# A hybrid layer on one core: three blocks between recurrence blocks, 64-row gate matmuls, and gate projections as paired seven-product blocks

## The chip, the cores and the metric

The kernel runs on one core of a Trainium2 chip. The metric is the device time of one execution in microseconds (us); shown are the median, the lowest and the highest of three executions, and one execution that was also recorded by the hardware profiler.

The engines are called PE (matrix multiplications), ACT (activation functions, copies and casts), DVE (element by element arithmetic and scans), POOL, and SP, which here only issues DMA transfers. An engine works through its own instructions in the order in which they stand in the program and waits at an instruction until the data that it needs are there.

## The reference

One layer is computed for 1024 latent tokens of width 1024 and 256 context tokens. Cut to what matters here:

```
h = rms_norm(x) * (1 + scale) + shift            # latents; the same for the context
u_lru, z_lru, u_fft, z_fft, u_pool, z_pool, gates = split(h @ w_in)
xc   = depthwise_conv(u_lru)                     # latents and context
r, i = sigmoid(block_diag(xc, wa)), sigmoid(block_diag(xc, wx))   # 64 x 64 blocks, two directions
a    = exp(-8 r softplus(-lam));  b = sqrt(1 - a^2) * (i * xc)
h_t  = a_t h_{t-1} + b_t                         # forward and backward, started by the context
ya = ((h_f + h_b) * silu(z_lru)) @ proj_a
yb = (fourier_mix(u_fft) * silu(z_fft)) @ proj_b
yc = (pool_mix(u_pool) * silu(z_pool)) @ proj_c
g  = sigmoid(gates)                              # three times 1024 columns: g, h, i
out = rms_norm(x + gate * ((g0 ya + g1 yb + g2 yc) @ w_out))
```

## The kernel before

**Tiling.** Channels lie on the 128 partitions, tokens along the free axis; a 128-channel block of 1024 tokens is one tile. Every fp32 operand of a product is split into a high and a low part (`split`, L127: ACT casts the high part, DVE subtracts for the low one), and `mm3` (L190 to L195) makes a product of three matmuls, low weight by high data, high by low, high by high. A projection block (eight 128-channel slices, 1024 tokens) is two half-blocks of 24 matmuls with 512 columns.

**Stages.** First come sums for the norm of x, the products `z` of L360 and the scaled activations: DVE scales `x` in place (`x<-x,gsc,rstd`), ACT makes the high part `hh`, DVE the low part `hl`; in between stand the splits of the last of these weights, `wz6` and `wz7`. Then a list `units` sets PE's order: four `ZP` blocks; eight recurrence blocks `u0` to `u7` with four other blocks behind each, from the list `others` (`UF`, `UP`, `ZF` and the 24 gate-logit blocks `i`, `h`, `g`); the last four gate blocks between the pooling products `m0` to `m3`; the branch products `c`, `s`, `t`, `b`, the blocks `pa` and the output product.

**A recurrence block.** `taken_in` makes the convolution `xc` (one ACT instruction and three on DVE, latents, and `xcc` for the context), `parts` its high and low parts (`xs`), and PE multiplies by the block-diagonal weights `bd`: `gates_c` (L701, context, tile `bdc`), then `gate` for r and i in each direction (`bdr`, `bdi`). In `parts` the high part of 64 channels lies above their low part, so one 128-row matmul does two of the three products. ACT takes sigmoids of all of them, exponentials, tanh and square roots, and each change between these kinds is an ACT_TABLE_LOAD. DVE multiplies and runs the scans (L768). The table `AT` (L1151) says at which half-block, counted from the block's own, each piece is written down:

```
AT = (("w", 0), ("in_", 1), ("sp", 1), ("gc", 4), ("g0r", 4), ("sc", 4), ("g0i", 5), ("s0r", 5), ("g1r", 6),
      ("s0i", 6), ("g1i", 7), ("s1r", 7), ("s1i", 8), ("ec", 8), ("e0", 8), ("e1", 8), ("qc", 8), ("q0", 8),
      ("q1", 8), ("kc", 8), ("k0", 8), ("z", 8), ("k1", 9), ("y", 9))
```

**Order.** PE's instructions run in the order in which they are written. ACT, DVE and SP follow an order that a scheduler made when the program was built; only in the start stage and at the end they too follow the code. All DMA transfers to and from memory are issued by SP in one row, so a store that waits for its data holds back the loads behind it.

Of the kernel before, what the change touches and what calls it, by code (L numbers as in the profile page):

```python
# [7 lines left out]
F32 = mybir.dt.float32  # L8
# [20 lines left out]
def tile_hybrid_mixer(  # L29
# [44 lines left out]
    def r4(name, shape=(128, 1024), pool=None):  # L74
        return (pool or p4).tile(list(shape), F32R, tag="t4", name=name)
# [141 lines left out]


    def hs(k, h):
        return tuple(t[:, h * HALF:(h + 1) * HALF] for t in ht[k])  # L220

    def proj_half(o, w, h, ks=range(NK), **kw):
# [19 lines left out]
    with tc.manual_schedule(engines={ET.PE}):  # L242
# [100 lines left out]

        def h_scaled(k):
            stt(xt[k], xt[k], gsc[0][k], rstd, ALU.mult, ALU.mult)
            ht[k] = r4(f"hh{k}"), r4(f"hl{k}")
            act(ht[k][0], xt[k], bias=shc[0][k])

        def h_lo(k):
            stt(ht[k][1], xt[k], shc[0][k], f(ht[k][0]), ALU.add, ALU.subtract)  # L350
            xt[k] = None


        def wave(k, ws, src):
            for n in range(3):
                for nm, hi, lo in ws:
                    o = pacc_t[nm]
                    for h in range(2):
                        x = src[k][n == 2][:, H[h]]
# [303 lines left out]
        def lru(j):  # L663
            t = lrus[j] = {}

            def weights():
                wf = f2(f"bd{j}_f", (128, 4, 128))
                SP.dma_start(out=wf, in_=bdw[j])
                t["wh"], t["wl"] = r2(f"bd{j}_h", (128, 4, 128)), r2(f"bd{j}_l", (128, 4, 128))
                split(t["wh"], t["wl"], wf)  # L670

            def taken_in():
# [2 lines left out]
                t["x"] = f4(f"xc{j}")  # L675
                conv(t["x"], t.pop("ps"), T, j)


            def stack(o, d, x):
                a, b = LANES[x], LANES[1 - x]  # L680
                S.copy(o[a], d[a])
                tt(o[b], d[a], f(o)[a], ALU.subtract)

            def parts():
                t["xc"] = r2(f"xs{j}", (128, 2, TC))
                for x in DIRS:
                    stack(t["xc"][:, x, :], t["c"], x)
                for x in DIRS:
                    t["xs", x] = r4(f"xs{j}_{x}")
                    stack(t["xs", x], t["x"], x)  # L690

            def both(o, n, x):
                for m, w in enumerate((t["wl"], t["wh"])):
                    PE.matmul(out=o, lhsT=w[:, n, :], rhs=x, start=m == 0, stop=m == 1)  # L694
# [5 lines left out]

            def gates_c():  # L701
                o = t["oc"] = acc(f"bdc{j}")
                cs = t.pop("xc")
                for n in range(4):
                    both(o[:, n * TC:(n + 1) * TC], 2 * (n % 2) + n // 2, cs[:, n % 2, :])

            def gate(x, kind):
                o = t["o", x, kind] = acc(f"bd{kind}{j}_{x}")
                for h in range(2):
                    both(o[:, H[h]], 2 * x + (kind == "i"), t["xs", x][:, H[h]])  # L710
                if kind == "i":
                    t.pop(("xs", x))

            def sigmoid_c():
                g, o = f4(f"gc{j}"), t.pop("oc")
                t["gc"] = g
                for n in range(4):
                    x, kind = n % 2, "ri"[n // 2]
                    for d in DIRS:
                        act(g[LANES[x], (2 * (n // 2) + d) * TC:(2 * (n // 2) + d + 1) * TC],  # L720
                            o[LANES[d], n * TC:(n + 1) * TC], AF.Sigmoid, bias=bias(x, kind)[LANES[d]])
# [57 lines left out]
            def gated():  # L779
# [7 lines left out]
            P = lambda f, *a: lambda: f(*a)  # L787
            return dict(w=weights, in_=taken_in, sp=parts, gc=gates_c, sc=sigmoid_c, ec=exp_c, qc=sqrt_c, kc=scan_c,
                        z=z_load, y=gated, e0=P(exp, 0), e1=P(exp, 1), q0=P(sqrt, 0), q1=P(sqrt, 1), k0=P(scan, 0),
                        k1=P(scan, 1), **{f"g{d}{k}": P(gate, d, k) for d in DIRS for k in "ri"},  # L790
                        **{f"s{d}{k}": P(sigmoid, d, k) for d in DIRS for k in "ri"})


# [328 lines left out]
        units += ("c0 c1 s0 c2 s1 t0 c3 s2 t1 c4 s3 t2 c5 t3 c6 c7 b0 b1 b2 b3 b4 b5 b6 b7").split()  # L1122
        units += halves(*[f"pa{n}" for n in range(NK)])
        pos_of = {u: n for n, u in enumerate(units)}
        wkeys = []
        for u in units:
            if isinstance(u, tuple):
                if u[1] == 0:
# [3 lines left out]
        queue = Queue([item(k) for k in wkeys])  # L1132
        branch = {"m": MP, "s": S1, "t": S2, "c": lambda d: PB(1, d), "b": lambda d: PB(0, d)}


# [7 lines left out]
        for k in range(NK):  # L1143
# [4 lines left out]
        on(6, ctx_parts, 0)  # L1148
        on(6, ctx_parts, 1)
        on(8, decays)  # L1150
        AT = (("w", 0), ("in_", 1), ("sp", 1), ("gc", 4), ("g0r", 4), ("sc", 4), ("g0i", 5), ("s0r", 5), ("g1r", 6),  # L1151
              ("s0i", 6), ("g1i", 7), ("s1r", 7), ("s1i", 8), ("ec", 8), ("e0", 8), ("e1", 8), ("qc", 8), ("q0", 8),
              ("q1", 8), ("kc", 8), ("k0", 8), ("z", 8), ("k1", 9), ("y", 9))
# [5 lines left out]
        on(pos_of["g4", 0] - 2, load_poolw)  # L1159
        on(pos_of["g4", 0], load_dft)  # L1160
        on(pos_of["g5", 0], group_dft)
# [5 lines left out]
        on(pos_of["g6", 0], load_tabs)  # L1167
        on(pos_of["g7", 0], split_tabs)
# [7 lines left out]
        on(pos_of["g4", 0] - 40, load_sbg)  # L1176
        for d in range(NK):
            on(pos_of["g4", 0] - 38 + 2 * d, gate_step, d)
        on(A0, load_ident)
        on(A0 + 2, gate_rows)  # L1180
        for k in range(3):
# [4 lines left out]
        for st, unit in enumerate(units):  # L1186
            flush_stores(st)
            late = st + 1
            for p in ev.pop(st, ()):
                p()  # L1190
            if isinstance(unit, tuple):
# [150 lines left out]
def _layout(i):  # L1342
# [4 lines left out]
    x, cx = a["x"][0], a["ctx"][0]  # L1347
    w = a["w_in"][0]

    bd = np.stack([a["lru_wa"][0], a["lru_wx"][0]]).reshape(2, 2, 8, 2, 64, 64).transpose(2, 4, 3, 0, 1, 5)  # L1350
    bd = np.concatenate([bd.reshape(8, 64, 4, 128)] * 2, axis=1)
# [42 lines left out]
```

## Time and profile before

| | |
|---|---|
| median of three executions | 1008.72 us (1008.42 to 1010.2) |
| the profiled execution | 1009.21 us, its span 1007.1 us |
| PE busy | 988.1 us, 4572 matmuls |
| DVE busy | 598.6 us |
| ACT busy | 537.3 us, of it 71 table loads 91.1 us |
| mean granted clock of PE | 0.997 |

The span is the recorded part of the execution, 2.1 us shorter than its time. A matmul's listed duration is longer than the distance to the next one, since matmuls overlap; the pace is read from the starts. A row "x2" is two instructions alike, with the time of both. In brackets stands the idle time of the engine ahead of an instruction and what ended it.

### The profile page before, as it was taken

To read this page: it belongs to the slowest core of one execution; us is meant where nothing else is said; L and a number is where in the kernel's file an instruction comes from. 1 tells how busy PE (TensorE), PEld (TensorE's weight loads), DVE (VectorE), ACT (ScalarE), POOL (GpSimd) and SP (SyncE) were. 2 spreads that over 40 slices of the span, in tenths; PEclk is the share of its full clock that TensorE was granted. 3 is DMA by queue.
4 is the path that set the end of the run, shared out by engine and by line. 5 is a ranking of instruction groups with operands and counts; after the bars stand their busy time and mean duration, and the time that the engine had idled before them with its cause. 6 is when DMAs were issued, how large, how long until landed. Compare 5 with 4: busy or idle time off the path is not lost.

```text
span 1007.1 us, 11592 instructions
## 1 busy us (share of the span) xinstructions
PE 988.1 (98%) x4572; PEld 816.9 (81%) x4572; DVE 598.6 (59%) x763; ACT 537.3 (53%) x632; POOL 21.6 (2%) x22
## 2 busy tenths in 40 slices
PE   7988999999999999999999999999999999999997
PEld 4867788888888888888888888887888888888886
DVE  6969266549465595653936537275566674456164
ACT  4453554595875948769596693954332222123031
POOL 0000000000000000000000000000000000000341
PEclk9999999999999999999999999999999999999999
DMA  9541495232322322334332233437545684324272
GB/s 341 210 157 43 147 411 237 73 105 84 109 90 94 105 96 88 137 140 147 136 138 92 74 105 136 135 118 283 170 173 212 244 318 157 138 83 136 73 250 75
DMA packets 47655, 152.58 MB, mean 152 GB/s; under 512 B 5489, under 2 KB 8177, under 8 KB 47602
## 3 DMA queue, kind: packets, MB, share of 16 engines
q1 hardware_dynamic: 47458, 151.59, 42.2%
q8 instruction: 36, 0.59, 0.2%
q10 hardware_dynamic: 144, 0.26, 0.1%
q14 instruction: 17, 0.14, 0.0%
HBM read 114.08 MB, written 37.75 MB: 151 GB/s over the span
## 4 chain that ended last, share of the span: by engine, by line
PE 82%; ACT 3%; DVE 2%; DMA 1%; issue 1%; SPq 0%; DVEq 0%; ACTq 0%
PE o L195 3%; PE o L194 3%; PE o L193 3%; PE ppa L195 3%; PE ph L194 3%; PE ppa L193 3%; PE ph L195 3%; PE pu L194 3%; PE pi L195 3%; PE ph L193 3%; PE pu L195 3%; PE pu L193 3%; PE pi L194 3%; PE pi L193 3%; PE ppa L194 3%; PE p L193 3%
## 5 line engine op out<-in xcount | busy, mean ns | idle before, releaser
L114 ACT ACT_TABLE_LOAD x71 | 91.1, 1283 | 2.0 <-PEq L1384 0.7
L120 DVE SCALAR_TENSOR_TENSOR junk<-ada,sb 128x1024 bf16<-128x1024 f32 x32 | 39.1, 1221 | 26.0 <-DMA ada<-in_ada 26.0
L194 PE MATMUL o<-wo_l,mh 128*128 128x512 f32 (+1 forms) x136 | 51.2, 377 | 0.0
L195 PE MATMUL o<-wo_h,mh 128*128 128x512 f32 (+1 forms) x136 | 51.2, 376 | 0.0
L193 PE MATMUL o<-wo_h,ml 128*128 128x512 f32 (+1 forms) x136 | 51.2, 376 | 0.0
L193 PE MATMUL pg<-hh,g_l 128*128 128x512 f32 x128 | 50.2, 392 | 0.0
L193 PE MATMUL ppa<-yh,pa_l 128*128 128x512 f32 x128 | 50.2, 392 | 0.0
L194 PE MATMUL ph<-hl,h_h 128*128 128x512 f32 x128 | 49.8, 389 | 0.0
L195 PE MATMUL ph<-hh,h_h 128*128 128x512 f32 x128 | 49.8, 389 | 0.0
L195 PE MATMUL ppa<-yh,pa_h 128*128 128x512 f32 x128 | 49.8, 389 | 0.0
L194 PE MATMUL pg<-hl,g_h 128*128 128x512 f32 x128 | 49.8, 389 | 0.0
L195 PE MATMUL pg<-hh,g_h 128*128 128x512 f32 x128 | 49.8, 389 | 0.0
L193 PE MATMUL ph<-hh,h_l 128*128 128x512 f32 x128 | 49.8, 389 | 0.0
L194 PE MATMUL ppa<-yl,pa_h 128*128 128x512 f32 x128 | 49.8, 389 | 0.0
L193 PE MATMUL pu<-hh,u_l 128*128 128x512 f32 x128 | 49.8, 389 | 0.0
L194 PE MATMUL pu<-hl,u_h 128*128 128x512 f32 x128 | 49.8, 389 | 0.0
L195 PE MATMUL pu<-hh,u_h 128*128 128x512 f32 x128 | 49.8, 389 | 0.0
L193 PE MATMUL pi<-hh,i_l 128*128 128x512 f32 x128 | 49.8, 389 | 0.0
L194 PE MATMUL pi<-hl,i_h 128*128 128x512 f32 x128 | 49.8, 389 | 0.0
L195 PE MATMUL pi<-hh,i_h 128*128 128x512 f32 x128 | 49.8, 389 | 0.0
L114 ACT ACTIVATE gc<-bdc,sml 64x256 f32<-64x256 f32 x64 | 30.0, 469 | 33.1 <-PE bdc L694 32.2
L117 DVE TENSOR_TENSOR i<-i,xc 128x1024 f32<-128x1024 f32 x16 | 18.9, 1224 | 44.7 <-ACT i L114 44.7
(387 smaller groups left out, 2649.0 us busy)
## 6 DMA issues: line engine op xcount, KB each, us to landing
ada<-in_ada SPq DMA_DIRECT2D x32, 512.0 KB, 8.4
x<-in_xT SPq DMA_DIRECT2D x8, 512.0 KB, 10.5
u_f<-in_w_in SPq DMA_DIRECT2D x8, 512.0 KB, 3.5
i_f<-in_w_in SPq DMA_DIRECT2D x8, 512.0 KB, 5.2
z<-k_z SPq DMA_DIRECT2D x8, 512.0 KB, 5.2
k_i<-ei SPq DMA_DIRECT2D x8, 512.0 KB, 2.7
k_y<-z SPq DMA_DIRECT2D x8, 512.0 KB, 2.6
h_f<-in_w_in SPq DMA_DIRECT2D x8, 512.0 KB, 4.8
```

What stands on the lines that cost most here:

```text
L114: S.activation(out=o, in_=i, func=func, **kw)
L117: V.tensor_tensor(o, a, b, op=op)
L120: V.scalar_tensor_tensor(o, a, s, b, op0=op0, op1=op1, **kw)
L193: PE.matmul(out=o, lhsT=wl, rhs=xh, start=first and i == 0, stop=False)
L194: PE.matmul(out=o, lhsT=wh, rhs=xl, start=False, stop=False)
L195: PE.matmul(out=o, lhsT=wh, rhs=xh, start=False, stop=last and i == n - 1)
```

## The change

It has three parts.

1. **Gates on 64 rows.** `parts` makes one split of all 128 channels, and `both` makes three matmuls for each half of 64 partitions, alternating between the two halves, which write different tiles. The context and r gates are written down at half-block 5 of a block, the i gates at 7.
2. **Three others per recurrence block.** 24 blocks instead of 32 lie in the recurrence, so eight half-blocks and no longer ten are written down for one block. `h4` to `h7` now lie between the pooling products.
3. **The g blocks in pairs.** Of two output blocks, two halves of the input channels and two halves of the tokens, seven products of 12 matmuls each take the place of eight (P1, P6, P2, P7, P5, P4, P3). They need sums of weight parts (`Pair.add`) and of activations (`mirror`). For the latter, ACT writes h in fp32 back into the `x` tile in the start stage, SP stores it (`hr`) and loads it again before the products.

With them `yc` is stored and loaded again, and the steps for the last gate (`load_sbg`, `gate_step`), the tables (`load_tabs`) and the weight queue of `pc`, `pb`, `pa` come later, at the branch products.

```diff
         def h_scaled(k):
             stt(xt[k], xt[k], gsc[0][k], rstd, ALU.mult, ALU.mult)
-            ht[k] = r4(f"hh{k}"), r4(f"hl{k}")
-            act(ht[k][0], xt[k], bias=shc[0][k])
+            ht[k] = r4(f"ha{k}"), r4(f"hb{k}")
+            if k < 4:
+                for h in range(2):
+                    act(hs(k, h)[0], xt[k][:, H[h]], bias=shc[0][k])
+            else:
+                act(ht[k][0], xt[k], bias=shc[0][k])
...
         def h_lo(k):
...
+            act(xt[k], xt[k], bias=shc[0][k])
+            keep(f"hr{k}", xt[k])
             xt[k] = None
...
+            def both(os, kind, xh, xl):
+                k = "ri".index(kind)
+                for n, (w, v) in enumerate(((t["wl"], xh), (t["wh"], xl), (t["wh"], xh))):
+                    for x in range(2):
+                        PE.matmul(out=os[x], lhsT=w[LANES[x], k, :], rhs=v[LANES[x]], start=n == 0, stop=n == 2)
...
+        def mirror(kk, a, b, make):
...
+            tt(v1, a1, a2, ALU.subtract)
+            put(1, v1)
+            stt(v2, v1, -1.0, b2, ALU.mult, ALU.subtract)
+            put(2, v2)
...
+            def product(self, p):
...
+                mm3(o, [(wh[:, kk], wl[:, kk]) + sums[FACTORS[p][1] + (kk,)] for kk in range(4)])
...
-        others = ("UF0 UP0 i0 i1 UF1 UP1 i2 i3 UF2 UP2 i4 i5 UF3 UP3 i6 i7 ZF0 ZF1 h0 h1 ZF2 ZF3 h2 h3 "
-                  "h4 h5 h6 h7 g0 g1 g2 g3 g4 g5 g6 g7").split()
+        others = ("UF0 UP0 i0 UF1 UP1 i1 UF2 UP2 i2 UF3 UP3 i3 ZF0 ZF1 i4 ZF2 ZF3 i5 i6 i7 h0 h1 h2 h3").split()
...
-            units += halves(f"u{j}", *others[4 * j:4 * j + 4])
-        units += halves("g4") + ["m0"] + halves("g5") + ["m1", "m2"] + halves("g6") + ["m3"] + halves("g7")
+            units += halves(f"u{j}", *others[3 * j:3 * j + 3])
+        units += halves("h4") + ["m0"] + halves("h5") + ["m1"] + halves("h6") + ["m2", "m3"] + halves("h7")
+        pairs = [Pair((f"g{n}", f"g{n + 1}")) for n in (0, 2, 4, 6)]
+        units += pair_units(len(pairs))
...
+        AT = (("w", 0), ("in_", 1), ("sp", 1), ("gc", 5), ("gr", 5), ("sc", 5), ("s0r", 5), ("s1r", 5),
+              ("gi", 7), ("s0i", 7), ("s1i", 7), ("ec", 8), ("e0", 8), ("e1", 8), ("qc", 8), ("q0", 8),
               ("q1", 8), ("kc", 8), ("k0", 8), ("z", 8), ("k1", 9), ("y", 9))
```

**DVE, end of recurrence block 2 and convolution of block 3.** `r2` and `i2` belong to block 2 (L768 is its scans), `xc3` and `xcc3` are the convolution of block 3, `i6` a weight. Before:

```order
L120 SCALAR_TENSOR_TENSOR r2_1_2451<-a2_1_2572,r2_1_2451 128x1024
...
L768 SCALAR_TENSOR_TENSOR i2_1_2492<-a2_1_2572,gc2_2392,r2_1_2451 128x1024
L117 TENSOR_TENSOR i2_0_2490<-i2_0_2490,i2_1_2492 128x1024
L117 TENSOR_TENSOR z2_2585<-z2_2585,i2_0_2490 128x1024
L120 SCALAR_TENSOR_TENSOR xc3_2713<-pu3_2634,sml_78,xc3_2713 128x1022
L120 SCALAR_TENSOR_TENSOR xc3_2713<-pu3_2634,sml_78,xc3_2713 128x1023
L134 TENSOR_TENSOR i6_l_2801<-i6_f_2729,i6_h_2800 128x1024
L120 SCALAR_TENSOR_TENSOR xcc3_2708<-cu3_2683,sml_78,xcc3_2708 128x254
L120 SCALAR_TENSOR_TENSOR xc3_2713<-pu3_2634,sml_78,xc3_2713 128x1023
```

Now the same place, with `xl3` the low part of the convolution:

```order
L117 TENSOR_TENSOR r2_1_2382<-r2_1_2382,i2_1_2461 128x1024
L120 SCALAR_TENSOR_TENSOR xc3_2587<-pu3_2479,sml_78,xc3_2587 128x1022
L782 SCALAR_TENSOR_TENSOR i2_0_2459<-a2_0_2509,gc2_2370,r2_0_2380 128x1024
L782 SCALAR_TENSOR_TENSOR i2_1_2461<-a2_1_2512,gc2_2370,r2_1_2382 128x1024
L134 TENSOR_TENSOR i3_l_2672<-i3_f_2600,i3_h_2671 128x1024
L120 SCALAR_TENSOR_TENSOR xcc3_2582<-cu3_2551,sml_78,xcc3_2582 128x254
L120 SCALAR_TENSOR_TENSOR xc3_2587<-pu3_2479,sml_78,xc3_2587 128x1023
L117 TENSOR_TENSOR i2_0_2459<-i2_0_2459,i2_1_2461 128x1024
L120 SCALAR_TENSOR_TENSOR xcc3_2582<-cu3_2551,sml_78,xcc3_2582 128x255
L120 SCALAR_TENSOR_TENSOR xc3_2587<-pu3_2479,sml_78,xc3_2587 128x1023
L117 TENSOR_TENSOR z2_2525<-z2_2525,i2_0_2459 128x1024
L120 SCALAR_TENSOR_TENSOR xcc3_2582<-cu3_2551,sml_78,xcc3_2582 128x255
```

The convolution's three long instructions still stand behind the products of the block before, now with its scans and sums between them.

**ACT, from the convolution of block 2 to its context gates.** `bdc2` is the product of the context gates on PE, `gc2` its sigmoids, `u3` and `UF3` weights, `pUF2` and `pUP2` finished products. Now:

```order
L114 ACTIVATE xc2_2188<-pu2_2080,sml_78 128x1024
L129 CAST i2_h_2272<-i2_f_2201 128x1024
L114 ACTIVATE xcc2_2183<-cu2_2152,sml_78 128x256
L129 CAST xh2_2196<-xc2_2188 128x1024
L129 CAST u3_h_2389<-u3_f_2270 128x1024
L881 COPY UF2_2256<-pUF2_2207 128x1024
L129 CAST xs2_2193<-xcc2_2183 128x256
L129 CAST UF3_h_2475<-UF3_f_2387 128x1024
L881 COPY UP2_2325<-pUP2_2276 128x1024
L114 ACT_TABLE_LOAD
L114 ACTIVATE gc2_2370<-bdc2_2343,sml_78 64x256 x8
```

The high part of the convolution is one cast `xh2` of 128 partitions instead of two of 64, and two casts, two copies and a table load stand between it and the sigmoids.

**ACT in the start stage.** Here are the instructions between the second and the fourth high part. Before:

```order
L114 ACTIVATE hh1_646<-x1_126,shc0_1_101 128x1024
L129 CAST wz6_h_652<-wz6_f_528 128x1024
L114 ACTIVATE hh2_657<-x2_127,shc0_2_102 128x1024
L114 ACTIVATE hh3_664<-x3_128,shc0_3_103 128x1024
L129 CAST wz7_h_670<-wz7_f_530 128x1024
```

Now:

```order
L114 ACTIVATE hb1_648<-x1_126,shc0_1_101 128x512
L114 ACTIVATE x0_125<-x0_125,shc0_0_100 128x1024
L129 CAST wz6_h_658<-wz6_f_528 128x1024
L114 ACTIVATE ha2_663<-x2_127,shc0_2_102 128x512
L114 ACTIVATE hb2_664<-x2_127,shc0_2_102 128x512
L114 ACTIVATE x1_126<-x1_126,shc0_1_101 128x1024
L114 ACTIVATE ha3_675<-x3_128,shc0_3_103 128x512
L114 ACTIVATE hb3_676<-x3_128,shc0_3_103 128x512
L114 ACTIVATE x2_127<-x2_127,shc0_2_102 128x1024
L129 CAST wz7_h_686<-wz7_f_530 128x1024
```

The writing back of `x0` and `x2`, which must come after DVE has read them for the low part, now stands ahead of the casts of `wz6` and `wz7`.

## Rows read from the trace of the kernel before

**Rows 1.** Part 1 of the page: busy time and instructions of each engine.

```profile
PE 988.1 (98%) x4572; PEld 816.9 (81%) x4572; DVE 598.6 (59%) x763; ACT 537.3 (53%) x632; POOL 21.6 (2%) x22
```

**Rows 2.** Windows: us, each engine's busy time (instructions), clock, DMA share, GB/s.

```profile
97.00:107.00 10.00, 7.71 (x51) 4.00 (x52) 10.00 (x16) 3.42 (x4) 0.00 (x0) 0.83 0.06 20
193.00:255.00 62.00, 62.00 (x290) 51.99 (x289) 37.38 (x45) 44.50 (x50) 0.00 (x0) 1.00 0.29 98
...
628.00:713.00 85.00, 83.45 (x366) 67.93 (x365) 43.34 (x41) 55.04 (x61) 0.00 (x0) 1.00 0.50 180
```

**Rows 3.** The chain that ended last (start us, us, what): gate products.

```profile
193.38 0.95 PE bdc L694 x8
...
200.71 0.91 PE bdi L694 x4
...
255.29 0.95 PE bdc L694 x8
```

**Rows 4.** Timeline of PE (start us, us, engine, line, operation) where the shape changes.

```profile
111.12 1.07 PE L360 MATMUL z<-hl,wz_h 128*128 128x512 f32 x4
112.12 1.50 PE L521 MATMUL psb<-ones,row 2*128 2x1 f32 x12
```

**Rows 5.** Timeline of PE in the start stage, three matmuls of one kind.

```profile
99.29 0.40 PE L505 MATMUL psb<-wc_h,shs 128*2 128x512 f32 x1 [2.53 <-DVE vz L117]
...
101.06 0.63 PE L505 MATMUL psb<-wc_l,shs 128*2 128x512 f32 x1
101.49 0.63 PE L505 MATMUL psb<-wc_h,shs 128*2 128x512 f32 x1
```

**Rows 6.** Timeline of ACT and DVE in the start stage.

```profile
74.65 1.04 ACT L129 CAST wz_h<-wz_f 128x1024 fp32r<-128x1024 f32 x1
76.05 1.22 DVE L134 TENSOR_TENSOR wz_l<-wz_f,wz_h 128x1024 fp32r<-128x1024 f32 x1
```

**Rows 7.** Timeline of ACT over one recurrence block.

```profile
256.28 3.86 ACT L114 ACTIVATE gc<-bdc,sml 64x256 f32<-64x256 f32 x8 [4.88 <-PE bdc L694]
260.16 1.28 ACT L114 ACT_TABLE_LOAD   x1
261.46 0.91 ACT L114 ACTIVATE ac<-gc,sc 128x256 f32<-128x256 f32 x2
265.00 0.63 ACT L114 ACTIVATE gc<-gc 128x512 f32<-128x512 f32 x1
...
279.14 2.19 ACT L114 ACTIVATE a<-r,sc 128x1024 f32<-128x1024 f32 x2
...
282.65 2.25 ACT L114 ACTIVATE i<-bdi,sml 64x1024 f32<-64x1024 f32 x2
...
288.43 2.01 ACT L114 ACTIVATE r<-r 128x1024 f32<-128x1024 f32 x2
...
298.01 1.21 ACT L114 ACTIVATE xc<-pu,sml 128x1024 f32<-128x1024 f32 x1 [4.29 <-PE pu L195]
300.65 1.06 ACT L129 CAST i_h<-i_f 128x1024 fp32r<-128x1024 f32 x1 [1.42 <-PE cu L193]
```

**Rows 8.** Timeline of DVE over the end of the same recurrence block.

```profile
289.52 2.36 DVE L120 SCALAR_TENSOR_TENSOR r<-a,r 128x1024 f32<-128x1024 f32 x2 [3.37 <-ACT r L114]
...
295.20 4.59 DVE L768 TENSOR_TENSOR_SCAN i<-a,gc,r 128x1024 f32<-128x1024 f32 x2
...
302.23 2.59 DVE L120 SCALAR_TENSOR_TENSOR xc<-pu,sml,xc 128x1022 f32<-128x1022 f32 x2
304.74 1.22 DVE L134 TENSOR_TENSOR i_l<-i_f,i_h 128x1024 fp32r<-128x1024 f32 x1
305.87 0.48 DVE L120 SCALAR_TENSOR_TENSOR xcc<-cu,sml,xcc 128x254 f32<-128x254 f32 x1
```

**Rows 9.** Part 6 of the page: DMA issues (size, us to landing).

```profile
z<-k_z SPq DMA_DIRECT2D x8, 512.0 KB, 5.2
```

More of the change, by code (lines that the diff above doesn't have):

```diff
@@ L676, in taken_in @@
                 conv(t["x"], t.pop("ps"), T, j)
[L679 to L682, printed above, removed]
             def parts():
[L685 to L694, printed above, removed]
+                cs = r2(f"xs{j}", (128, 2, TC))
+                t["ch"], t["cl"] = cs[:, 0, :], cs[:, 1, :]
+                split(t["ch"], t["cl"], t["c"])
+                t["xh"], t["xl"] = r4(f"xh{j}"), r4(f"xl{j}")
+                split(t["xh"], t["xl"], t["x"])
+            def both(os, kind, xh, xl):
[3 more added lines that the diff above has]
+                        PE.matmul(out=os[x], lhsT=w[LANES[x], k, :], rhs=v[LANES[x]], start=n == 0, stop=n == 2)
             def bias(x, kind):
@@ L702, in gates_c, with gate @@
                 o = t["oc"] = acc(f"bdc{j}")
[L703 to L708, printed above, removed]
+                ch_, cl_ = t.pop("ch"), t.pop("cl")
+                for k in range(2):
+                    both([o[:, x * HALF + k * TC:x * HALF + (k + 1) * TC] for x in range(2)], "ri"[k], ch_, cl_)
+            def gate(kind):
+                os = [acc(f"bd{kind}{j}_{x}") for x in range(2)]
+                for x in range(2):
+                    t["o", x, kind] = os[x]
                 for h in range(2):
-                    both(o[:, H[h]], 2 * x + (kind == "i"), t["xs", x][:, H[h]])
+                    both([o[:, H[h]] for o in os], kind, t["xh"][:, H[h]], t["xl"][:, H[h]])
                 if kind == "i":
-                    t.pop(("xs", x))
+                    for k in ("xh", "xl", "wh", "wl"):
+                        t.pop(k)
             def sigmoid_c():
@@ new lines, in mirror_h, with __init__, load, add @@
+        def mirror_h(kk):
+            a, b = (fetch(f"hr{k}", f4(f"hr{k}")) for k in (kk, kk + 4))
+            mirror(kk, a, b, lambda n: r4(f"hs{n}"))
+            for v, q in ((1, (kk, 0)), (2, (kk + 4, 0)), (3, (kk + 4, 1))):
+                sums["b", v, kk] = hs(*q)
+        FACTORS = {"P1": ("a11", ("b", 1)), "P6": ("s2", (2,)), "P2": ("a12", ("b", 2)), "P7": ("s3", (3,)),
+                   "P5": ("s1", (1,)), "P4": ("a22", (4,)), "P3": ("s4", ("b", 3))}
+        class Pair:
+            def __init__(self, keys):
+                self.keys, self.w = keys, {}
+                self.raw = []
+            def load(self):
+                for k in self.keys:
+                    self.raw.append(f4(k + "_f", KK, praw))
+                    SP.dma_start(out=self.raw[-1], in_=item(k)[1])
+            def add(self):
+                a, b = self.raw
+                r = self.r = dict(a11=a[:, 0:4], a12=a[:, 4:8], a22=b[:, 4:8])
+                for n in range(1, 5):
+                    r[f"s{n}"] = f2(f"{self.keys[0]}s{n}", (128, 4, 128))
+                tt(r["s1"], b[:, 0:4], b[:, 4:8], ALU.add)
+                tt(r["s2"], r["s1"], a[:, 0:4], ALU.add)
+                tt(r["s3"], a[:, 0:4], b[:, 0:4], ALU.add)
+                tt(r["s4"], a[:, 4:8], r["s2"], ALU.add)
+                self.raw = None
+            def parts(self, p):
+                n = FACTORS[p][0]
+                t = r4(self.keys[0] + n, (128, 2, 4, 128), pwt)
+                self.w[p] = t[:, 0], t[:, 1]
+                split(t[:, 0], t[:, 1], self.r.pop(n))
+            def product(self, p):
+                n, r = divmod(banks["n"], 4)
+                if r == 0:
+                    banks["t"] = [None] * 2
+                if r < 2:
+                    banks["t"][r] = acc(f"b{n}_{r}")
+                o = banks["t"][r % 2][:, H[r // 2]]
+                banks["n"] += 1
+                wh, wl = self.w.pop(p)
+                mm3(o, [(wh[:, kk], wl[:, kk]) + sums[FACTORS[p][1] + (kk,)] for kk in range(4)])
+                if p == "P1":
+                    self.e = [f4("e" + k) for k in self.keys]
+                (a0, a1), (b0, b1) = ([e[:, h] for h in H] for e in self.e)
+                if p == "P1":
+                    S.copy(a0, o)
+                elif p == "P6":
+                    tt(a1, a0, o, ALU.add)
+                elif p == "P2":
+                    tt(a0, a0, o, ALU.add)
+                elif p == "P7":
+                    tt(b1, a1, o, ALU.add)
+                elif p == "P5":
+                    tt(a1, a1, o, ALU.add)
+                    self.o5 = o
+                elif p == "P4":
+                    tt(b0, b1, o, ALU.add)
+                    tt(b1, b1, self.o5, ALU.add)
+                    self.o5 = None
+                    act(self.e[1], self.e[1], AF.Sigmoid, scale=-1.0)
+                    keep(self.keys[1], self.e[1])
+                else:
+                    tt(a1, a1, o, ALU.add)
+                    act(self.e[0], self.e[0], AF.Sigmoid)
+                    keep(self.keys[0], self.e[0])
+                    self.e = None
@@ L875, in tile_hybrid_mixer, with pair_units @@
+        banks = dict(n=0)
+        def pair_units(pairs):
+            return [(p, n) for n in range(pairs) for p in FACTORS]
         tabs = {}
@@ L1157, in tile_hybrid_mixer @@
                 on(LRU_AT[j] + n, pieces[k], table=ev if k == "w" else aft)
-        on(pos_of["g4", 0] - 2, load_poolw)
-        on(pos_of["g4", 0], load_dft)
-        on(pos_of["g5", 0], group_dft)
+        W0, C0 = pos_of["P1", 0], pos_of["c0"]
+        for (p, n), at in [(u, pos_of[u]) for u in units if u[0] in FACTORS]:
+            if p == "P1":
+                on(at - 9, pairs[n].load)
+                on(at - 5, pairs[n].add)
+            on(at - 4, pairs[n].parts, p)
+        for kk in range(4):
+            on(W0 - 8 + 2 * kk, mirror_h, kk)
+        on(pos_of["h4", 0] - 2, load_poolw)
+        on(pos_of["h6", 0], load_dft)
+        on(pos_of["h7", 0], group_dft)
+        for g in range(4):
+            on(C0 - 5 + g, load_c, g)
         for n in range(4):
@@ L1190, in tile_hybrid_mixer @@
                 p()
-            if isinstance(unit, tuple):
+            if isinstance(unit, tuple) and unit[0] in FACTORS:
+                if st == C0 - 2:
+                    queue = queues[1]
+                    queue.start()
+                pairs[unit[1]].product(unit[0])
+            elif isinstance(unit, tuple):
                 half_block(*unit)
```

58 lines of the change are left out of this document (41 added, 17 removed).

## The prediction

> **What bounds the kernel now.** The page's busy times come first: PE works 988.1 of 1007.1 us, so the span is PE's work and little else [rows 1]. The windows say the same of the stages that the change rebuilds: in a recurrence block PE is busy for all 62.00 us, DVE for 37.38 and ACT for 44.50; behind the recurrence, from 628 to 713 us, PE for 83.45 of 85 [rows 2]. The chain of the end gives prices. From one block's context gates to the next's are 255.29 - 193.38 = 61.9 us; four 512-column matmuls take 0.91, eight 256-column ones 0.95, thus 0.227 and 0.119 us each [rows 3]. A half-block is 24 x 0.227 = 5.45 us, a block 10.9. In the start stage DVE is the full engine, 10.00 of 10 us, and PE waits 2.53 us for it [rows 2, 5]. Last, the timelines of ACT and DVE over one block show what the shares hide: a row of instructions each of which needs the one before, from the context gates' sigmoids to the next block's convolution [rows 7, 8]. ACT waits 4.88 us for `bdc` and 4.29 for `pu` on that way: today this row has room.
>
> **Products.** Seven for eight leaves out 4 x 12 = 48 matmuls of 512 columns: -10.9 us [rows 3]. The sums are 16 on DVE for the activations and four per pair, with casts and subtractions; a pair lasts 7 x 12 x 0.227 = 19.1 us on PE, and its own DVE work is about 18 instructions of 512 columns at some 0.65 (half of the 1.22 for 1024, an estimate from [rows 8]), 12 us. That is hidden in the pairs themselves; ahead of the first pair it isn't, below.
>
> **Gates.** Before: 16 matmuls of 512 columns and 8 of 256 per block, 36.7 us in eight blocks. Now 24 and 12, of half the rows. No row shows a 64-row matmul. If two halves run side by side, a pair costs one matmul: 27.5 us, -9.2. If one after the other: 55.0, +18.3. The two halves have rows of the array and output tiles of their own; I take side by side and keep both ends. The nearest row on a change of shape is four matmuls that begin at 111.12 and give way at 112.12 to a 2-row one: 1.00 instead of 0.91, 0.09 more [rows 4]. Two stretches of gates per block are 32 changes: +3. The Trainium skill, "TensorEngine Tiling (Array Packing)", Key Properties, states that tiles work in parallel and that a change of tiling mode drains the engine. By the first statement the gates give -9.2; the row of 0.09 agrees with a small price for the second, and no row here shows the first.
>
> **Start stage.** DVE's `wz_l` began at 76.05, and its cast had run at 74.65: no wait [rows 6]. Now ACT writes `x0` back ahead of that cast, and may do so only when DVE has read `x0` for the low part, which stands directly ahead of `wz_l`. DVE thus waits for the writing (about 1.2, as one ACT instruction of 1024 columns from PSUM [rows 7]) and the cast (1.04 [rows 6]), 2.2 us, and again at `wz7`. Small steps fill a part. DVE sets PE's start at 99.29 [rows 5]: +4, between 0 (other work fills it) and 5.
>
> **The recurrence.** With three others, PE needs per block 8 x 5.45, the context's 24 x 0.119 and the gates: 43.6 + 2.9 + 3.4 + 0.4 for the changes of shape = 50.3 us. The order now decides whether ACT and DVE can follow. Count from S, the start of the eight context sigmoids, with the prices of [rows 7, 8], on ACT: sigmoids 3.86, the cast of `bd` 0.3 (a quarter of 1.04), r 2 x 2.25, table load 1.28, exponential and tanh 2 x 0.91, load 1.28, square root 0.63, a cast 1.04, load 1.28, evacuation of `pi` 1.06, i 2.25, load, a 2.19, load, i 2.25, tanh 2.2, load, the first square root 1.0: S + 30.8. Nothing on this way waits; it is ACT's own work. The second square root and `xc` end at S + 33.0. DVE meanwhile waits for the square root as it did at 289.52, and then does r 2.36, r x i 2.4, the first `xc` 1.3, two scans 4.59, a weight 1.22, `xcc` 0.48, the second `xc` 1.3, the sum 1.22, `xcc` 0.48, the third `xc` 1.3: S + 47.4. Only now can ACT cast `xh`, and behind it stand in ACT's order a weight, the copy `UF`, the small `xs`, a weight, the copy `UP` and a table load: five of 1.05, 0.4 and 1.28 make 54.4, less some 0.7 because listed durations overlap by about 0.1 (300.65 + 1.06 against the next start). The next S comes **53.7 us** after the last. On PE `bdc` needs the low part `xs`, four DVE steps behind `xh`, and ends at about S + 53: both ends meet. From the blocks with `Z` on, evacuations need one or two table loads more (1.28 each) ahead of the sigmoids: I count 55.4, 56.4, 55.1 and 55.3. Seven periods are 383.3 us; PE alone would need 352.1. **+31.** This holds whether or not the halves run side by side: one after the other PE needs 43.6 + 2.9 + 6.9 + 0.4 = 53.8, and the +31 becomes +7 while -9.2 becomes +18.3, 3 us worse in all. What is late next is everything behind the last block.
>
> **Behind the recurrence.** From the last S, ACT has 28 us of work and nine table loads (11.5) up to the cast of the pooled input of `m1`: S + 39.6; DVE makes the low part behind scans' inputs at about S + 44.6. PE has done `h3`, the i gates, `h4`, `m0` and `h5` at about S + 35.5: a wait of 9. `m2`'s input is a load that SP issues only behind the store of the last `y`, at about S + 51, plus 5.2 to land [rows 9]: 2 us. `m3`'s cast stands on ACT behind seven casts for the mirrored sums and pair 0, which want two loads from the same row of SP: about S + 71 against 60: 10. Together about +20. Kept ends: 0 (the loads come in time and the order leaves no gap) and 25 (after such waits PE runs slower for a while: after 2.53 us of waiting one kind of matmul went at 0.43 us, the granted clock of the window was 0.83, which is time at 1.2 instead of 2.4 GHz [rows 2, 5]). In the recurrence that costs nothing of its own while ACT and DVE set the pace.
>
> **Sum.** -10.9 - 9.2 + 3 + 4 + 31 + 20 = +38 on the profiled 1009.21, which is 0.5 above the median: about **1047 us**. The steps moved behind `c0` (`gate_step`, tables) cost nothing as long as PE has its blocks there; eight DVE steps of 1.22 are 10 us in a stage of some 280, and if they had no cover they would cost these 10.
>
> **Rivals.**
> (1) The recurrence is bound as I say, but behind it PE finds its inputs: 1009.2 - 10.9 - 9.2 + 3 + 4 + 31 and 0 to 8 = 1027 to 1035. For it: ACT has idle time in no row of mine there, but SP's order is only known, not timed. 0.19.
> (2) Faster: DVE and ACT keep up, so that PE sets the pace through. It needs the third `xc` by S + 44 instead of 47.4, 3.4 us earlier per block, with side by side gates: 1009.2 - 10.9 - 9.2 + 3 + 0 to 4 = 992 to 996, and up to 1006 where some waits stay. Against it: every instruction on the way is listed in order and has its price in a row. 0.13.
> (3) The halves run one after the other: +18.3 and +7 for -9.2 and +31, 1050. It is the likeliest case but for 3 us; 0.17 of its chance.
> (4) Gains and waits cancel, 1006 to 1011: 0.04.
>
> **Numbers.** My case with (3) has 0.62, its own range 1036 to 1060; above that 0.02. The range 1012 to 1060 leaves out (2), (4) and that tail, under 0.2. Three executions lay within 0.2%, and a smaller difference can't be told: faster 0.14, same 0.03, slower 0.83.
>
> **What would show it.** The starts of `bdc` should lie 53 to 57 us apart, not 50.3, with PE waiting for DVE's `xs` or `xl` once per block for about 3 us; if they lie 50 apart, the count on ACT and DVE is wrong. Gate matmuls of 512 columns should begin in pairs 0.227 us apart; 0.227 between any two of them means one after the other. PE should wait longer than 2.53 us for `vz`, and at `m1` and `m3` for `ph` or `pl` about 9 and 10 us. Wrong would make me a DVE or ACT that reaches `xc` earlier than its row of instructions allows, for example by shorter sigmoids or table loads.

## The result

The changed kernel takes 1073.09 us (1071.19 to 1074.92), the kernel before 1008.86 beside it: 1.0641 times as long, 95% interval 1.0628 to 1.0655. The sign was forecast, the size wasn't: 1047 us were predicted, 1060 at most.

Part 1 of the page of the changed kernel, busy time and instructions of each engine, answers to [rows 1]:

```profile
PE 1001.1 (93%) x4620; PEld 813.5 (76%) x4620; DVE 636.5 (59%) x847; ACT 553.7 (52%) x670; POOL 21.6 (2%) x22
```

PE has 13 us more of listed time although 48 matmuls of 512 columns went (the gates brought 96 more, of 64 rows), and it now idles for 72 of 1073.1 us. Windows of the changed kernel (columns as in [rows 2]: one recurrence block, from the last context gates to the first product, the products, the branch products, the `pa` blocks):

```profile
256.00:310.00 54.00, 52.38 (x252) 42.83 (x252) 34.29 (x47) 39.77 (x47) 0.00 (x0) 0.97 0.26 91
...
585.00:681.00 96.00, 74.02 (x305) 57.21 (x306) 57.51 (x70) 59.89 (x74) 0.00 (x0) 0.86 0.55 190
681.00:766.00 85.00, 78.54 (x338) 63.94 (x337) 48.08 (x70) 30.53 (x42) 0.00 (x0) 0.98 0.39 134
766.00:879.00 113.00, 112.21 (x600) 96.76 (x600) 82.04 (x111) 35.46 (x45) 0.00 (x0) 1.00 0.71 259
879.00:980.00 101.00, 92.64 (x391) 74.53 (x390) 47.20 (x41) 18.95 (x19) 0.00 (x0) 0.95 0.41 147
```

The third number from the end is the granted clock: 0.97 in a recurrence block and 0.86 ahead of the products; in [rows 2] it is 1.00 in the same two stages. Of the five stretches only the branch products run as before (113.3 us instead of 112.9). The waits of PE in the changed kernel (who was waited for, us in total, times, longest):

```profile
PE mp L193 <- ACT ph L129: 11.7, 2, 10.2
PE bdc L704 <- ACT xs L129: 10.0, 6, 3.3
PE mp L194 <- DVE pl L134: 7.2, 2, 4.7
PE ppa L193 <- ACT yh L129: 7.1, 2, 4.5
PE b L193 <- DVE eg L117: 6.5, 3, 3.7
PE bdc L704 <- DVE xs L134: 6.4, 4, 1.7
...
PE psb L518 <- DVE vz L117: 3.3, 1, 3.3
```

Now PE at the gates, to be held against [rows 3]:

```profile
309.76 0.39 PE L704 MATMUL bdc<-xs,bd 64*128 64x256 f32 x2 [0.35 <-ACT xs L129]
311.85 1.43 PE L704 MATMUL bdc<-xs,bd 64*128 64x256 f32 x10 [1.71 <-DVE xs L134]
313.08 0.63 PE L704 MATMUL bdr<-xh,bd 64*128 64x512 f32 x2
313.51 0.63 PE L704 MATMUL bdr<-xl,bd 64*128 64x512 f32 x2
```

And the window behind these waits:

```profile
312.00:314.80 2.80, 2.80 (x20) 2.40 (x22) 2.80 (x7) 2.28 (x5) 0.00 (x0) 0.50 0.51 200
```

PE waits 0.35 us for ACT's `xs`, begins `bdc`, waits 1.71 us for DVE's `xs` and goes on at half clock: the granted clock is 0.50, and two 64-row matmuls of 512 columns take 0.43 us, against 0.24 in `gates64_alone` below. The context gates of the eight blocks begin at 202.6 and then 52.6 to 56.1 us apart, up to 584.9. The row of ACT that leads there, against [rows 7]:

```profile
258.74 3.88 ACT L114 ACTIVATE gc<-bdc,sml 64x256 f32<-64x256 f32 x8 [0.47 <-PE bdc L704]
...
263.64 0.41 ACT L129 CAST bd<-bd_f 128x256 fp32r<-128x256 f32 x1 [1.01 <-DMA bd_f<-in_bdw]
...
291.60 1.21 ACT L114 ACTIVATE xc<-pu,sml 128x1024 f32<-128x1024 f32 x1
...
306.49 1.05 ACT L129 CAST xh<-xc 128x1024 fp32r<-128x1024 f32 x1 [12.28 <-DVE xc L120]
```

From the sigmoids at 258.74 ACT works to 294.2 with one pause of 1.01 us, for the load of `bd`, then waits 12.28 us for DVE's third `xc` before it can cast `xh`. DVE in the same block, against [rows 8]:

```profile
290.65 2.36 DVE L120 SCALAR_TENSOR_TENSOR r<-a,r 128x1024 f32<-128x1024 f32 x2 [3.37 <-ACT r L114]
...
296.39 4.59 DVE L782 TENSOR_TENSOR_SCAN i<-a,gc,r 128x1024 f32<-128x1024 f32 x2
...
305.11 1.28 DVE L120 SCALAR_TENSOR_TENSOR xc<-pu,sml,xc 128x1023 f32<-128x1023 f32 x1
...
311.37 0.43 DVE L134 TENSOR_TENSOR xs<-xcc,xs 128x256 fp32r<-128x256 f32 x1
```

The third `xc` begins at 305.11, behind products and scans of the block before, as the order has it.

In the start stage ACT of the changed kernel writes `x0` back ahead of the cast of `wz6`, against [rows 6]:

```profile
77.07 1.15 ACT L114 ACTIVATE x<-x,shc 128x1024 f32<-128x1024 f32 x1 [1.26 <-DVE hb L120]
78.12 1.03 ACT L129 CAST wz_h<-wz_f 128x1024 fp32r<-128x1024 f32 x1
```

PE's `psb` products begin at 104.76 instead of 99.29 [rows 5], 5.5 us later. They take 5.6 us instead of the 7.2 before, where part of them ran at half clock [rows 5], so PE is 3.9 us late at the first projection block (122.98 instead of 119.11).

**Where the 66 us of the span come from**, by PE's marks in the two traces and the prediction's price of PE's own work: 3.9 in the start stage; 382.3 us from the first to the last context gates, where PE alone needs 352 by the prediction, 30; 96.0 from the last context gates to the first product, where it needs some 66 (five blocks of 10.9, the gates 4.3, four pooling products of 1.4, `pq` 1.3), 30; 85.0 for 28 products that need 76.3, 9; 100.9 in the `pa` blocks instead of 88.8, 12. Together 85; against that stands the work that went, some 17 by the prediction's prices (10.9 for the products, 6 for the gates). That makes 68; of the 2 too many, 1.6 are PE's own waits at the pooling products of the kernel before (0.8 twice).

### The profile page after: what moved, and what is told of

Its sections match the earlier page's. It is cut to its first block, busy times and chain, and to the rows that moved or that the text cites. A ratio compares the mean times of both kernels' runs of the same rounds, so it can differ in the third digit from the quotient of the medians.

```text
span 1073.1 us, 11872 instructions
## 1 busy us (share of the span) xinstructions
PE 1001.1 (93%) x4620; PEld 813.5 (76%) x4620; DVE 636.5 (59%) x847; ACT 553.7 (52%) x670; POOL 21.6 (2%) x22
## 4 chain that ended last, share of the span: by engine, by line
PE 41%; ACT 23%; DVE 12%; issue 8%; DMA 6%; SPq 0%; DVEq 0%; ACTq 0%
ACT r L114 6%; ACT L114 5%; ACT i L114 3%; PE o L193 3%; PE o L194 3%; PE o L195 3%; ACT gc L114 3%; PE ppa L194 3%; PE ppa L195 3%; PE ppa L193 3%; DVE i L782 2%; PE b L193 2%; PE b L195 2%; PE b L194 2%; PE p L194 2%
## 5 line engine op out<-in xcount | busy, mean ns | idle before, releaser
L117 DVE TENSOR_TENSOR i<-i,xc 128x1024 f32<-128x1024 f32 x16 | 18.9, 1224 | 58.9 <-ACT i L114 58.9
L193 PE MATMUL ph<-ha,h_l 128*128 128x512 f32 x96 | 40.0, 416 | 1.9 <-ACT eh L114 1.9
L193 PE MATMUL pi<-ha,i_l 128*128 128x512 f32 x96 | 38.4, 400 | 0.0
L195 PE MATMUL ph<-ha,h_h 128*128 128x512 f32 x96 | 38.2, 398 | 0.0
L193 PE MATMUL pu<-ha,u_l 128*128 128x512 f32 x96 | 38.2, 397 | 0.0
L195 PE MATMUL pi<-ha,i_h 128*128 128x512 f32 x96 | 37.6, 392 | 0.0
L194 PE MATMUL ph<-hb,h_h 128*128 128x512 f32 x96 | 37.4, 389 | 0.0
L195 PE MATMUL pu<-ha,u_h 128*128 128x512 f32 x96 | 37.4, 389 | 0.0
L194 PE MATMUL pu<-hb,u_h 128*128 128x512 f32 x96 | 37.3, 389 | 0.0
L194 PE MATMUL pi<-hb,i_h 128*128 128x512 f32 x96 | 37.3, 389 | 0.0
L782 DVE TENSOR_TENSOR_SCAN i<-a,gc,r 128x1024 f32<-128x1024 f32 x16 | 36.9, 2340 | 0.0
L120 DVE SCALAR_TENSOR_TENSOR r<-a,r 128x1024 f32<-128x1024 f32 x16 | 18.9, 1223 | 29.3 <-ACT r L114 29.3
```

Of the source, the lines that this page charges most:

```text
L193: PE.matmul(out=o, lhsT=wl, rhs=xh, start=first and i == 0, stop=False)
L194: PE.matmul(out=o, lhsT=wh, rhs=xl, start=False, stop=False)
L195: PE.matmul(out=o, lhsT=wh, rhs=xh, start=False, stop=last and i == n - 1)
L782: V.tensor_tensor_scan(o[:, w], a[:, w], b[:, w], s, op0=ALU.mult, op1=ALU.add)
```

## The experiments

Times of a kernel are held against the runs of the kernel before on the same chip (1008.1 to 1008.5).

**The convolution first.** The later pieces of a block are written down behind the next block's convolution:

```diff
-              ("gi", 7), ("s0i", 7), ("s1i", 7), ("ec", 8), ("e0", 8), ("e1", 8), ("qc", 8), ("q0", 8),
-              ("q1", 8), ("kc", 8), ("k0", 8), ("z", 8), ("k1", 9), ("y", 9))
+              ("gi", 7), ("s0i", 7), ("s1i", 7), ("ec", 10), ("e0", 10), ("e1", 10), ("qc", 10), ("q0", 10),
+              ("q1", 10), ("kc", 10), ("k0", 10), ("z", 10), ("k1", 11), ("y", 11))
```

> The changed kernel, but the exponentials, square roots and scans of a recurrence block are written down two half-blocks later, behind the next block's convolution, so that ACT and DVE make the convolution first. Theory (the row of ACT and DVE instructions from the sigmoids over the scans to the convolution sets the 53.6 to 56 us of a recurrence block): the distance of the context gates on PE falls to about 50.3 us, PE's waits for xs go, and 28 to 34 us are gained: 1037 to 1045 us. Rival (PE sets the pace itself, by 64-row matmuls, changes of shape or a lower clock): the distance stays above 53 us and the time above 1066.

Measured: 1052.22 us, ratio 1.0443 (1.0425 to 1.0460), 21 us less than the changed kernel. ACT of this kernel, between the sigmoids at 261 and the next at 313:

```profile
280.71 1.20 ACT L114 ACTIVATE xc<-pu,sml 128x1024 f32<-128x1024 f32 x1 [4.74 <-PE pu L195]
...
287.35 1.05 ACT L129 CAST xh<-xc 128x1024 fp32r<-128x1024 f32 x1 [2.49 <-DVE xc L120]
```

The convolution now waits for PE's `pu` (4.74), `xh` only 2.49 for DVE, and the exponentials follow. DVE has the low part `xs` at 290.0:

```profile
289.58 0.42 DVE L134 TENSOR_TENSOR xs<-xcc,xs 128x256 fp32r<-128x256 f32 x1
```

PE's waits for `xs` are gone; the context gates begin at 253.29 and again at 305.26, 52.0 us apart:

```profile
253.29 0.98 PE L704 MATMUL bdc<-xs,bd 64*128 64x256 f32 x12
```

From the first to the last of them 361.2 us pass instead of 382.3, which is the whole gain. The theory holds and the rival falls, though 28 to 34 us were expected. The distance is not the 50.3 that I reckoned for PE alone: in five of the blocks PE now waits some 0.6 us at `pu` or `pi` for ACT, the changes of shape cost more than I put in (next), and 2 to 3 of the 9 us by which the seven distances exceed my count stay without a cause. The order also spares table loads, 48 of them instead of 73. That alone, 25 x 1.28 us or some 4 us a block, isn't why the wait went: `xs` is now ready 15 us before PE takes it.

**The 64-row gates alone**, in the kernel before (the functions of the change's first part and its `AT`, four others between blocks, ordinary g blocks):

> The kernel before with the 64-row gates alone (four others between recurrence blocks, no paired products). Theory (halves run side by side, a change of shape costs about 0.1 us, and with four others PE has 61.2 us of work against 53.7 on ACT and DVE): 1002 to 1004 us, distance of the context gates 61.2 to 61.4. Rival 1 (changes of shape cost several tenths each or the halves run one after the other): at or above 1009. Rival 2 (ACT and DVE bind here too): 1009 or more, with PE waiting for xs.

Measured: 1010.52 us, 1.0021 (1.0011 to 1.0030): slower by 2 us, where both rivals had put it. PE at one block's gates:

```profile
259.30 0.39 PE L195 MATMUL pUP<-hh,UP_h 128*128 128x512 f32 x1
259.62 0.98 PE L692 MATMUL bdc<-xs,bd 64*128 64x256 f32 x12
260.43 0.40 PE L692 MATMUL bdr<-xh,bd 64*128 64x512 f32 x2
260.67 0.40 PE L692 MATMUL bdr<-xl,bd 64*128 64x512 f32 x2
...
261.92 0.50 PE L193 MATMUL pi<-hh,i_l 128*128 128x512 f32 x1
262.25 0.40 PE L194 MATMUL pi<-hl,i_h 128*128 128x512 f32 x1
```

From 259.30, the start of the last 128-row matmul, to 261.92, the start of the next one behind the gates, are 2.62 us; less that matmul's 0.23, and with 0.10 because the matmul behind it comes 0.33 and not 0.23 later, the stretch costs 2.49. The stretch of the i gates costs 1.78 in the same way (272.73 to 274.63). Together 4.27 a block. The work without changes of shape is 6 x 0.119 + 12 x 0.227 = 3.44, so four changes cost 0.83, **0.21 each** and not 0.09. In the kernel before the gates of a block cost 1.88 + 3 x 0.91 = 4.61. The gain is thus 0.34 a block, and the distance of the context gates fell from 61.9 to 61.7. Rival 1 is thus right in part: a change costs twice what I gave it, but the gates still gain. Rival 2 falls, since PE waits for no `xs`. The gain is lost at `m1`, where PE now waits longer (0.8 before):

```profile
PE mp L193 <- ACT ph L129: 4.6, 1, 4.6
```

That pairs run side by side is shown by the rows at 260.43 and 260.67: two matmuls of 512 columns every 0.24 us, where a single 128-row one takes 0.23. The statement of the Trainium skill, "TensorEngine Tiling (Array Packing)", Key Properties, that different tiles work in parallel, agrees with these rows, and its other statement, that a change of mode drains the engine, fits the 0.21 us that a change costs; the rows don't show the drain itself.

**Three others alone**, in the kernel before, with its 128-row gates:

```diff
...
-            units += halves(f"u{j}", *others[4 * j:4 * j + 4])
+            units += halves(f"u{j}", *others[3 * j:3 * j + 3])
+        units += halves("h4", "h5", "h6", "h7", "g0", "g1", "g2", "g3")
```

> The kernel before with three others per recurrence block alone: its 128-row gates and ordinary g blocks, with h4 to h7 and g0 to g3 behind the recurrence, ahead of the blocks with the pooling products. PE's work is that of before. Theory (the row of instructions on ACT and DVE sets the pace as soon as there are eight half-blocks per block; the stacked halves make it some 2 us longer than in the changed kernel): context gates 55 to 58 us apart and 1036 to 1050 us. Rival (the 64-row gates or the pairs made the recurrence slow): gates 51 to 52 us apart and at most 1012 us.

Measured: 1057.92 us, 1.0490 (1.0475 to 1.0504), more than I expected and far from the rival. PE waits for DVE once per block:

```profile
PE bdc L694 <- DVE xs L117: 35.5, 7, 8.6
```

```profile
304.99 0.55 PE L694 MATMUL bdc<-xs,bd_l 128*128 128x256 f32 x1 [4.00 <-DVE xs L117]
```

The context gates begin 57.4 us apart here (247.63 to 304.99), and 55.5 to 62.6 over the eight blocks. PE's work for a block is 61.9 - 10.9 = 51.0. From 192.13 to 600.02 are 407.9 us, 51 more than seven times that: all of the 49.5 us arise in the recurrence. Two of the steps for the last gate stand on DVE ahead of the low part of `xcc` in the block with the longest wait (8.6 us).

**No pairs.** The changed kernel without the paired products; PE has 10.9 us more to do:

> The changed kernel without the paired products: g0 to g7 are ordinary blocks behind h7, and the writing back of h, its stores and loads and all sums are gone. PE then has 48 matmuls of 512 columns more, 10.9 us. Theory (the steps that the pairs need cost PE more than they save: about 4.5 us in the start stage, some 13 at m3, 6.5 in the pairs, and half clock behind): 1050 to 1060 us, the distance of the context gates unchanged at 53.6 to 56. Rival (the waits at m1 and m3 come from the recurrence block alone and stay): 1070 to 1084.

Measured: 1057.25 us, 1.0475 (1.0456 to 1.0493). Some of PE's waits in this kernel:

```profile
PE mp L194 <- DVE pl L134: 5.3, 2, 4.7
...
PE mp L193 <- ACT ph L129: 3.4, 2, 2.0
```

`psb` begins at 99.78, 5 us earlier than in the changed kernel; at `m3` 2.6 us are left of 12.7, and at `m1` 6.1 as in the changed kernel. The pairs cost 15.8 us more than they save, as the theory had it.

**Pooling inputs early.**

```diff
-            on(pos_of[f"m{n}"] - 3, load_pool, n)
+            on(pos_of[f"m{n}"] - (3, 5, 7, 8)[n], load_pool, n)
```

> The changed kernel with the inputs of the pooling products m1 to m3 loaded and cast up to five half-blocks earlier. Theory (PE's waits of 6 and 13 us at m1 and m3 come from the order on ACT and SP, and PE at half clock behind them adds a few us): 1051 to 1058 us. Rival (the waits move on to the products, whose activation sums come from the same row of loads): 1064 to 1072.

Measured: 1059.90 us, 1.0520 (1.0500 to 1.0540), 13 us less. The waits at `m1` and `m3` (18.9 us) are gone, but PE waits at the next place, `pq`, for ACT's evacuation of a block:

```profile
PE pq L1032 <- ACT eh L114: 11.1, 1, 11.1
```

Both theories have a part: the order made the waits, and 11 of 19 us only moved.

**The last gate's steps back in the recurrence**, from 40 units ahead of `h4` on, as the kernel before has them from 40 units ahead of `g4` on:

> The changed kernel with the loads and sums for the last gate (load_sbg, gate_step) written down in the recurrence again, as before. Theory (these 4 MB of loads in SP's row delay the loads of y, for which PE waits 8 us in the pa blocks, and half clock behind it): 1060 to 1064 us. Rival 1 (the loads of y are late for another reason): 1070 to 1074. Rival 2 (eight DVE steps of 1.3 us go on the row of DVE instructions that sets the recurrence): 1066 to 1072, with the pa blocks mended and the distance of the context gates longer by up to 1.3 us.

Measured: 1067.69 us, 1.0594 (1.0577 to 1.0612), 5.4 us less. No wait in the `pa` blocks is left, and they take 88.8 us again. So the loads of these steps did delay those of `y`: the last of the latter is issued 6.8 us ahead of the first `pa` block here, and 5.0 behind it in the changed kernel, while they take 7.2 us (median) to land in both. Whether SP's row alone held them back, or the tiles too that both kinds of load fill, isn't separated. Some 1.8 us of the gain lie in the start stage, which the edit doesn't touch. The recurrence pays: from the first to the last context gates are 388.6 us instead of 382.3, and PE's waits there rise:

```profile
PE bdc L704 <- ACT xs L129: 14.8, 6, 4.4
...
PE bdc L704 <- DVE xs L134: 7.6, 4, 2.8
```

Rival 2 was right, with a larger price.

**Mended versions.** Four edits together (convolution first, pooling inputs early, gate steps back, and h written back only at the end of the start stage):

> The changed kernel with four edits together: the exponentials to scans behind the next convolution, the pooling inputs early, the last gate's loads back in the recurrence, and h written back into the x tiles only behind the last low part of the start stage. Theory (the waits are independent, each goes with its edit): the first wait of PE for vz falls to about 2.5 us or less and the context gates begin 4 us earlier, the distance is 51 to 52 us, the waits at the pa blocks are gone; a wait before the products stays, since the sums' loads still stand in SP's row: 1016 to 1030 us. Rival (the waits only change places): above 1040.

Measured: 1029.79 us, 1.0215 (1.0200 to 1.0231). Within the range; but the fourth edit gained nothing. `psb` begins at 101.91, 2.9 us earlier than in the changed kernel, but behind a longer wait for `vz` (5.0 us; DVE now waited 2.03 us for a store of `hr`), and its matmuls then go at half clock and take 8.3 us instead of 5.6; the context gates began at 202.5 as before. And a small table came late:

```profile
PE pq L1036 <- DMA fw<-in_gw: 12.8, 1, 12.8
...
PE psb L520 <- DVE vz L117: 5.0, 1, 5.0
```

Then these two places and the split of the pairs' weights were mended too (`h_back` one step behind the casts, `load_dft` at `h4`, weights of P2 one product earlier):

> As four_mended, with three places mended that its profile showed: in the start stage h is written back one step behind the casts of wz6 and wz7 (not all at the end), the two small tables of the channel transform are loaded four units earlier (PE waited 12.8 us for one of them), and of each pair the second product's weights are split one product earlier, so that the raw weights of the pair after next can come sooner. Theory (each of these is a wait by order and buffers alone): context gates begin 3 to 4.5 us earlier, no wait at the transform, 2 to 3 us less in the pairs: 1006 to 1014 us. Rival (the waits change places once more): 1018 us or more.

Measured: 1025.40 us, 1.0162 (1.0144 to 1.0181): the rival's side. The context gates begin 4.6 us earlier (197.89), but PE now waits at `pq` for ACT, and longer again at `h7` and the products:

```profile
PE pq L1037 <- ACT eh L114: 7.1, 1, 7.1
```

With `pq` at `h6`:

```diff
-        on(pos_of["h7", 0], group_dft)
+        on(pos_of["h6", 0], group_dft)
```

> five_mended with the channel transform's product (pq) two units earlier, at h6. Theory (PE's 7 us there were a wait for a PSUM tile that ACT frees behind the casts of the sums): the wait at pq goes and some of it comes back at h7 or the first pair, where the same ACT row is waited for: 1018 to 1023 us. Rival (it all comes back): 1024 to 1027.

Measured: 1025.15 us, 1.0174 (1.0158 to 1.0189): it all came back, now at `m` and (3.8 us) at `h7`, behind the same evacuations `eh` on ACT:

```profile
PE mp L193 <- ACT eh L114: 7.0, 1, 7.0
```

ACT ahead of that `eh`, and the window around it (columns as in [rows 2]):

```profile
615.07 0.62 ACT L129 CAST hs<-s 128x512 fp32r<-128x512 f32 x1 [4.61 <-DVE s L120]
618.51 1.21 ACT L129 CAST hs<-s 128x512 fp32r<-128x512 f32 x2 [2.83 <-DVE s L120]
...
621.03 1.02 ACT L114 ACTIVATE eh<-ph 128x1024 f32<-128x1024 f32 x1
...
610.00:622.00 12.00, 5.15 (x23) 3.94 (x21) 12.00 (x13) 4.54 (x6) 0.00 (x0) 0.90 0.36 131
```

ACT isn't full here: it works 4.54 of 12.00 us and waits 4.61 and 2.83 for DVE's sums `s`, while DVE works all of the 12.00. The product that `eh` takes in was finished by 613.8, since PE's last matmul of an `h` block ahead of it began at 613.40. The evacuation thus waits for its place in ACT's order, behind casts that wait for DVE. In front of these casts it could begin some 6 us earlier (an estimate from 613.8 and a table load of 1.28, against 621.03); that order wasn't tried.

**A version that beats both.** gates64_alone with the pooling inputs earlier:

```diff
-            on(pos_of[f"m{n}"] - 3, load_pool, n)
+            on(pos_of[f"m{n}"] - (4, 5, 5, 5)[n], load_pool, n)
```

> gates64_alone with the inputs of the pooling products loaded and cast one to two units earlier. Theory (the 64-row gates save about 2 us of PE and lost it to a wait of 4.6 us at m1, which is the order on ACT): the wait at m1 falls to 0 to 2 us, 1005.5 to 1008 us, faster than before by 0.1 to 0.3%. Rival (the wait stays or moves to m2): 1009 to 1011.

Measured: 1003.55 us, 0.9959 (0.9946 to 0.9972), 0.4% faster than the kernel before and 2 us below what I expected, for which I have no cause. The wait at `m1` is gone; of PE's waits at the pooling products this is left:

```profile
PE mp L193 <- DVE zp L120: 0.5, 1, 0.5
```

## Why the prediction was right and wrong

**The recurrence was right.** The forecast "**53.7 us** after the last" and "383.3 us" for seven periods stand against 382.3, and the row of instructions came as counted: from the sigmoids at 258.74 DVE's first product behind the square root began at S + 31.9 (30.8 counted; the 1.01 us for the load of `bd` are most of the difference), and the third `xc` ended at S + 47.6 (47.4). That the sum of the seven fits within 1 us is in part luck: the single distances are 52.6 to 56.1 and miss the count by up to 2.7. The 352.1 us for PE alone were 9 too low, as the 361.2 of `conv_first` show; while ACT and DVE set the pace, that cost nothing. That the order causes it is shown by `conv_first`, which changes only the order, and that the eight half-blocks are enough for it by `three_others_alone`.

**The start stage was right:** +4 forecast, +5.5 at `psb`, 5 of it gone without the writing back (`no_pairs`), and +3.9 at the first projection block. DVE waited as forecast for the second of the two casts, 2.15 us, and 0.19 for the first.

**The gates were mis-sized.** "-9.2" for matmuls side by side is right, "+3" for 32 changes of shape is 6.7: the one row I used showed the entry into another shape (0.09), not what the second matmul behind it loses (0.10). Since the recurrence waits for ACT and DVE, this cost nothing in the changed kernel.

**Behind the recurrence, "+20" was too small.** PE's waits at `m1`, `m2` and `m3` are 6.1, 0 and 12.7 us, 18.9 in all, where 9, 2 and 10 were counted: the sum fits better than its terms. The other 11 of the 30 had no term: 3 are waits of 1.3 and 1.9 us at `bdc` and `ph`, and 8 are slower matmuls, since PE is busy for 74.0 us with work that needs 66. The end that I kept for it, 25, was too low too: I took one row on the clock [rows 5] as a few us in all, where the mean granted clock over these 96 us is 0.86.

**"That is hidden in the pairs themselves" failed.** I held 12 us of DVE work against 19.1 of PE and overlooked the order: at the end of the first pair the additions `eg` that PE waits for stand on DVE among four sums for a later pair (`g4s`), the first of which itself waited 0.50 us for its load:

```profile
696.54 0.69 DVE L117 TENSOR_TENSOR g4s<-g_f 128x512 f32<-128x512 f32 x1 [0.50 <-DMA g_f<-in_w_in]
...
700.28 0.68 DVE L117 TENSOR_TENSOR eg<-eg,b 128x512 f32<-128x512 f32 x1
701.02 0.80 PE L193 MATMUL b<-ha,g0s 128*128 128x512 f32 x1 [3.69 <-DVE eg L117]
```

PE waits 6.5 us in three places in all (`b<-DVE eg`), and with the clock the stage is 9 us longer. Splitting the weights earlier, in `five_mended`, changed nothing here (6.0 us as in `four_mended`); that the order of the additions alone would end them wasn't tried.

**"The steps moved behind `c0` cost nothing" failed,** with 12 us. I priced their DVE work against PE's cover and kept 10 us as the other end, but never as part of the range. The mechanism is a different one: their 4 MB of loads stand in SP's row ahead of and between the loads of `y`, as `gate_steps_back` shows. Two terms set at nothing were thus 21 us; with the 10 us that were missing behind the recurrence they are 31, against 28 by which the span of the changed kernel exceeds the forecast for the profiled execution (1045).

**Still open:** how the 30 us ahead of the first product split into waits that a better order would end and the work on the sums itself. Three edits each moved the wait to the next place, and none ended it. In `six_mended` DVE is full where PE waits, so its work there has no cover; ACT isn't, and part of PE's wait may be its order alone, which is not shown.

## What to carry to other kernels

A busy share of 53 and 59% for the helpers hid a row of dependent instructions of 54 us per 62 us block; before one shortens the stage that covers such a row, one adds the row up in program order and compares it with what is left of the cover. When work is put into stages at the end of another, every DMA it issues and every buffer it waits for is in the price, not its arithmetic alone. Where a wait is mended and comes back at the next place, one looks whether the engine that is waited for is full there or itself waits in its order: here ACT had idle time, and DVE behind it had none.

## What the runs showed of the hardware

Two 64-row matmuls on different halves begin within 0.01 us of each other; the timeline of PE in `five_mended`, at a place where PSUM held them up:

```profile
262.91 0.49 PE L709 MATMUL bdi<-xh,bd 64*128 64x512 f32 x1 [0.32 <-ACT r L114]
262.92 0.72 PE L709 MATMUL bdi<-xl,bd 64*128 64x512 f32 x2
```

By the program's order the first row is the second half's matmul of one pair, and the second row begins with the first half's matmul of the next pair. A change between 128-row and 64-row matmuls cost 0.21 us, counted on both sides. And short waits are dear: behind a wait of 1.71 us at `bdc` (0.35 us stood ahead of it) pairs of matmuls of the changed kernel went at 0.43 us instead of 0.24 until 314.8, some 3 us, at a granted clock of 0.50, the lower of the two levels (1.2 instead of 2.4 GHz).
